# A two-layer diffusion step on one core: parameter loads on ScalarE's queue, the second layer's gate rows through DRAM, and a slack in the order of four kinds of products

## The chip, the cores and the metric

The kernel runs on one core of a Trainium2 chip. The metric is the time of one execution on the device, in microseconds (us). Three runs of the kernel before took 2245.87 us in the median (2241.98 to 2256.99).

## The reference, cut to what matters

Two token sets, 1024 noisy tokens and 256 context tokens, each 1024 wide, go through two layers. Everything is float32.

```
mod   = silu(cond) @ w_ada[layer] + b_ada[layer]       # shift, scale, gate; cond is c or c_ctx
h     = rmsnorm(x, norm_g[layer]) * (1 + scale) + shift
# layer 0: RWKV-7 scan in both directions beside a gated 3-tap convolution
proj  = h @ w_in_e                                     # 1024 x 4352
kk    = k * k_k; kk = kk / max(sqrt(sum_head(kk * kk)), 1e-12)
S     = S * w_t - (S kk_t) (kk_t a_t)^T + v_t k_t^T    # per head 64 x 64, every token, forward and backward
y     = y_f + y_b
y     = (y - mean_head(y)) * rsqrt(var_head(y) + GN_EPS) * lnx_g + lnx_b
bonus = sum_head(r * mean(k_dir) * r_k) * v
x     = x + gate0 * (concat(((y + bonus) * silu(g_a)), conv_branch) @ w_out_e)
# layer 1: grouped-query attention, 16 query heads of 64 on 4 key heads, 512 cached context keys,
# rotary positions, softmax, a SiLU gate on the heads
x     = x + gate1 * ((softmax(q k^T / 8) v * silu(g)) @ w_out_o)
y     = rmsnorm(x, final_g)
```

The gates are vectors of 1024 numbers, one for each token set and layer.

## The kernel before, in words

All values that TensorE multiplies in the large products are split into two float32r parts (`hi`, `lo`), so that each product is three matmuls. The work runs in five stages that overlap at their edges.

1. **Start.** SyncE's queue loads the two conditioning vectors (`crow`), eight tiles of 1 MiB of the first layer's `w_ada` (`wada`, five buffers), four tiles of tokens of 512 KiB (`xt`), and twelve small parameter arrays into the rows of two tiles `prow`, which TensorE turns into columns (`par`). ScalarE forms `cond` from the conditioning vectors; TensorE multiplies it with each `wada` tile as it lands. VectorE turns the sum into the modulation columns (`mod`).
2. **First layer.** The input projection (`mm<-h_hi,whi` and its two companions, weights in pieces of 128 by 128) runs beside the scan. The scan is cut into 20 steps, five for each of four head pairs: four groups of 256 noisy tokens and one for the context. A step is prepared (`prepare`), its triangular systems are built (`interact`), solved on VectorE by 31 pairs of small operations on `acc` and `tmp` (`solve`), put together on TensorE (`merge`) after a trip of the solution through DRAM (`w_d`), and then run through the chain of four blocks (`chain`, tiles `ch`, `py`, `hv`). `close_groups` then normalises y, with the sum over a head as a matmul with the constant `ones2`: once for the mean (operand `y`), once for the squares (operand `sqy`). `norm_k` does the same for the squares of k (operand `sq`), `bonus` for the bonus (operand `kds`).
3. **First output projection** (`Proj` of layer 0, `proj0`): TensorE takes token rows (`omh`) times `w_out_e` (`wts`); VectorE multiplies the result with a gate row (`og<-mm,row`), GpSimd adds x. Behind it comes the turned and modulated h of layer 1 (`all_h1`).
4. **Second layer.** Products with `w_in_o`, then the attention: for each of 24 pairs (two heads, a block of tokens) the scores `qh,kh`, their exponentials on ScalarE (`pe`), the products with the values (`pv<-pe,v_sb`), and the sums of the exponentials (`zs`, on GpSimd and VectorE), which two matmuls add over the partitions (`wk<-zs,twos`).
5. **Second output projection** (`proj1`), the last norm and the stores.

**A gate row** is the gate vector spread over all 128 partitions. `all_rows` makes half of one (512 numbers) at a time, four for a layer: four VectorE operations scale the identity with the gate columns into `dg`, one matmul with the constant `minus` spreads it, and VectorE or ScalarE copies it to `row`.

**What sets the order.** A recording layer (`Loom`) runs all these pieces as generators. Each names what it needs next (`yield "T", operands, rings`), and the loom, with its own costs for the engines, takes the first in a list of precedence (`PRECEDENCE`) that its estimate says could start soon, else the one that could start earliest. What it takes is written into the engines' queues in that order, and the chip runs each queue in order. A need may carry a number, which for an engine other than TensorE is how long another piece may be late to be taken first. The loom works only from the end of the start on; the start is in the order of the program and a priority for the large loads. A `Ring` is a set of buffers that are taken and released; `wk_ps` has two PSUM banks, and one during the attention, since the other goes to the scores. A pool of buffers is opened when the one before is closed: `op0` serves `proj0`, `op1` serves `proj1`.

Names and lines of the kernel before: the loom's `when` is at line 315, the parameter loads at 425 to 446, `norm_k` at 724, `bonus` at 891, `close_groups` at 1253, `all_moved` (the pools) at 1495, `open_proj` at 1602, `all_rows` at 1688. In the profile almost every instruction bears line 145, the loom's own, so they are told apart by the names of their tiles.

Of the kernel before, what the change touches and what calls it, by code (L numbers as in the profile page):

```python
# [17 lines left out]
P = 128  # L18
# [98 lines left out]
class Loom:  # L117
# [199 lines left out]
    def when(self, need):  # L317

        if callable(need):
            return self.clock["T"] if need() else None  # L320
        engines, items, rings, _ = need
        t0 = 0.0
        for x, m in rings.items():
            t = x.ready(m)
            if t is None:
                return None
            t0 = max(t0, t)
        return min(max([t0, self.clock[e]] + [self.free(e, x) for x in items]) for e in engines)

# [38 lines left out]
def hybrid_step(  # L368
# [54 lines left out]
    with tc.tile_pool(name="prm", bufs=2, reuse_waits="tile") as prm:  # L423
        with tc.high_priority():
            crow = prm.tile([16, P], F32, name="crow", bufs=1)
            for i, x in enumerate((c.rearrange("o (n p) -> (o n) p", p=P), c_ctx.rearrange("(n p) -> n p", p=P))):
                dma(out=crow[8 * i:8 * i + 8, :], in_=x)
            pt = py_ps()
            T.transpose(out=pt[:, 0:16], in_=crow, identity=ident[0:16, 0:16])
            V.tensor_copy(par[:, 0:16], pt[:, 0:16])  # L430
        rows["c"], rows["c_ctx"] = 0, 8
        r0 = 0
        t0 = 16
        cur = prm.tile([P, P], F32, tag="prow", name="prow")
        for name, ap, n in specs:
            if r0 + n > P:
                pt = wk_ps()
                T.transpose(out=pt[:, 0:r0], in_=cur[0:r0, :], identity=ident[0:r0, 0:r0])
                V.tensor_copy(par[:, t0:t0 + r0], pt[:, 0:r0])
                t0 += r0  # L440
                r0 = 0
                cur = prm.tile([P, P], F32, tag="prow", name="prow")
            dma(out=cur[r0:r0 + n, :], in_=ap)
            rows[name] = t0 + r0
            r0 += n
        pt = wk_ps()
        T.transpose(out=pt[:, 0:r0], in_=cur[0:r0, :], identity=ident[0:r0, 0:r0])
        V.tensor_copy(par[:, t0:t0 + r0], pt[:, 0:r0])
# [278 lines left out]
    def norm_k(p, b, f, done):  # L727

        t0, n, _ = BLK[b]
        for h in range(0, n, GRP):  # L730
# [3 lines left out]
            S.activation(sq, fh, AF.Square, scale=col("k_k", p))  # L734
            yield "T", sq, wk_ps
            pt = wk_ps.take()
# [158 lines left out]
    def bonus(p, t0, t):  # L895
        yield lambda: passed[f"v{p}"]
        v = st1.tile([P, GRP], F32, tag="vb", name="vb")
        dma(out=v, in_=sp[p][:, 3, t0:t0 + GRP])
        yield "T", t, wk_ps
        pm = wk_ps.take()  # L900
# [352 lines left out]
    def close_groups(x, p, gs):  # L1253
        yield lambda: passed[f"g{p}"]
        sqs, side = [], []
        for t0, y in gs:
# [3 lines left out]
            dma(out=sgt, in_=sg_d[p][:, t0:t0 + GRP])  # L1260
            yield "T", y, iv_ps
            pm = iv_ps.take()
# [6 lines left out]
            S.activation(sq, y, AF.Square)  # L1269
            yield "T", sq, iv_ps  # L1270
            pm = iv_ps.take()
# [201 lines left out]
    k_d = dram.tile([4, NT, C], F32, name="k_d")  # L1473
    v_d = dram.tile([NT, 256], F32, name="v_d")
    m_d = dram.tile([24, P, 32], F32, name="m_d")
    rz_d = dram.tile([24, 2, 512], F32, name="rz_d")
# [22 lines left out]
    def idle(*names):  # L1499
        return not any(R[name].busy for name in names)  # L1500

    def all_moved():
# [26 lines left out]
        close_pool("nx")  # L1529
        yield lambda: len(x1_made) == 2 * N and idle("om", "omh", "og", "xr", "row")  # L1530
        close_pool("op0")
# [70 lines left out]
    def open_proj(name, halves, rows):  # L1602
# [5 lines left out]
        ring(p, "row", [P, 512], rows)  # L1608
        ring(p, "dg", [P, 512], 1)
        if name == "op1":  # L1610
# [28 lines left out]
    def all_wsplit():  # L1639
        for _ in range(len(parts) * KT):  # L1640
# [5 lines left out]
            R["wraw2"].release(raw)  # L1646
            ws[name].append((hi, lo))


    class Proj:  # L1650
# [38 lines left out]
        def all_rows(self):  # L1689
# [3 lines left out]
            for i, h in self.todo:  # L1693
# [3 lines left out]
                seen.append((cd, h))  # L1697
                yield "V", R["dg"], R["row"]
                dg = R["dg"].take()
                row = R["row"].take()  # L1700
                for s in range(4):
                    V.tensor_scalar(out=dg[:, s * P:(s + 1) * P], in0=ident,
                                    scalar1=mods[self.l][:, 16 + h * 4 + s, cd:cd + 1], scalar2=-1.0, op0=ALU.mult, op1=ALU.mult)
                yield "T", dg, wk_ps
                pt = wk_ps.take()
                T.matmul(pt, fixed["minus"], dg, start=True, stop=True)
                R["dg"].release(dg)
                yield from copied(pt, (row, pt))
                wk_ps.release(pt)
                self.rows[cd, h] = row  # L1710
# [694 lines left out]
    def om1_there(i):  # L2405
# [3 lines left out]

    named = dict(chained=all_chained, merged=all_merged, solved=lambda: all_solved(0), solved1=lambda: all_solved(1), finished=all_finished, evac=evacuate,  # L2410
                 loaded=all_loaded, split=all_split, interacted=all_interacted, prepared=all_prepared, x=all_x, h0=lambda: all_h(0), h1=lambda: all_h(1), ada=all_ada,
# [54 lines left out]
```

## Time and profile before

| | |
|---|---|
| median of three runs | 2245.87 us |
| the profiled execution | 2246.71 us |
| its span, first to last instruction | 2245.1 us |
| mean granted TensorE clock | 0.956 of 2.4 GHz |
| TensorE busy | 2044.0 us, 91% |
| VectorE, ScalarE, GpSimd busy | 66%, 47%, 45% |
| moved by DMA | 104 GB/s in the mean |

By the trace, TensorE's first product with a weight of `w_ada` starts at 25 us, the scan runs from 250 to 1167 us, the input projection ends at 1109 us, the first output projection and the products of the second layer fill 1168 to 1523 us, the attention runs to 2126 us, and the last product ends at 2237 us. One reads such a profile by its gaps: 91% busy is a mean over stages, and a gap that one stage has can be filled only by what is ready in that stage. A busy share at a granted clock below 1.00 is also longer than it need be.

### The profile page before, as it was taken

To read this page: it belongs to the slowest core of one execution; us is meant where nothing else is said; L and a number is where in the kernel's file an instruction comes from. 1 tells how busy PE (TensorE), PEld (TensorE's weight loads), DVE (VectorE), ACT (ScalarE), POOL (GpSimd) and SP (SyncE) were. 2 spreads that over 40 slices of the span, in tenths; PEclk is the share of its full clock that TensorE was granted. 3 is DMA by queue.
4 is the path that set the end of the run, shared out by engine and by line. 5 is a ranking of instruction groups with operands and counts; after the bars stand their busy time and mean duration, and the time that the engine had idled before them with its cause. 6 is when DMAs were issued, how large, how long until landed. Compare 5 with 4: busy or idle time off the path is not lost.

```text
span 2245.1 us, 42922 instructions
## 1 busy us (share of the span) xinstructions
PE 2044.0 (91%) x15307; PEld 1406.8 (63%) x15307; DVE 1476.1 (66%) x3483; ACT 1050.0 (47%) x2475; POOL 1013.6 (45%) x1153
## 2 busy tenths in 40 slices
PE   4898889898989999898879999999999999999898
PEld 1486666676666666666657688886544444454487
DVE  3346978858787887878745733555677767775443
ACT  3446647545555456554435632221444444444422
POOL 2434444333344343433224321330587777888622
PEclk8999999899998999999989999999999999999899
DMA  7824434323334343342355633322321211112143
GB/s 290 288 92 137 115 96 125 91 68 107 100 95 108 88 103 93 91 118 54 86 161 183 202 110 90 96 86 89 105 55 45 63 40 36 45 28 75 55 132 107
DMA packets 337817, 232.85 MB, mean 104 GB/s; under 512 B 163890, under 2 KB 289860, under 8 KB 335556
## 3 DMA queue, kind: packets, MB, share of 16 engines
q1 hardware_dynamic: 337604, 230.12, 35.1%
q8 instruction: 120, 1.97, 0.4%
q14 instruction: 93, 0.76, 0.1%
HBM read 166.95 MB, written 57.75 MB: 100 GB/s over the span
## 4 chain that ended last, share of the span: by engine, by line
PE 38%; DVE 10%; DMA 5%; issue 3%; ACT 1%; SPq 1%; POOL 1%; DVEq 0%; POOLq 0%; ACTq 0%
PE mm L145 21%; PE pv L145 8%; PE py L145 5%; PE wk L145 4%; DVE mx L145 3%; DVE rz L145 2%; DVE zs L145 1%; DMA rz<-rz_d 1%; DVE tmp L145 1%; DVE acc L145 1%; SPq L145 1%; DMA rz_d<-rc 1%; PE ch L145 1%; DMA om<-om_d 1%; DVE wts L145 0%
## 5 line engine op out<-in xcount | busy, mean ns | idle before, releaser
L145 POOL TENSOR_TENSOR zs<-zs,pe 128x512 f32<-128x512 f32 x276 | 368.7, 1368 | 43.3 <-ACT pe L145 41.7
L145 PE MATMUL mm<-h_hi,whi 128*128 128x512 f32 (+1 forms) x816 | 336.5, 412 | 4.1 <-ACT whi L145 3.9
L145 PE MATMUL mm<-h_hi,wlo 128*128 128x512 f32 (+1 forms) x816 | 299.1, 366 | 12.6 <-DVE wlo L145 11.7
L145 PE MATMUL mm<-h_lo,whi 128*128 128x512 f32 (+1 forms) x816 | 298.2, 365 | 0.0
L145 POOL TENSOR_TENSOR wlo<-wraw,whi 128x128 fp32r<-128x128 f32 x228 | 110.6, 491 | 242.1 <-ACT whi L145 196.3
L145 PE MATMUL pv<-pe,v_sb 128*64 128x512 f32 (+1 forms) x832 | 203.2, 611 | 0.0
L145 PEld LDWEIGHTS mm<-h_hi,whi 128*128 128x128 f32 x816 | 159.4, 195 | 49.6 <-issue 13.4
L145 PEld LDWEIGHTS mm<-h_hi,wlo 128*128 128x128 f32 x816 | 159.9, 196 | 41.0 <-DVE wlo L145 14.1
L145 DVE TENSOR_TENSOR acc<-acc,tmp 128x60 f32<-128x60 f32 (+23 forms) x620 | 166.9, 271 | 21.0 <-issue 3.1
L145 PEld LDWEIGHTS mm<-h_lo,whi 128*128 128x128 f32 x816 | 160.9, 197 | 14.4
L145 PE MATMUL mm<-wts,omh 128*128 128x512 f32 x624 | 161.0, 409 | 9.1 <-ACT wts L145 5.9
L145 PE MATMUL mm<-wts,h_hi 128*128 128x512 f32 x480 | 151.1, 396 | 0.0
L145 POOL TENSOR_TENSOR hg<-hv,gc 64x128 f32<-64x128 f32 x152 | 65.5, 431 | 188.9 <-DVE hv L145 177.7
L145 DVE TENSOR_REDUCE mx<-py 128x1 f32<-128x512 f32 (+1 forms) x173 | 111.0, 661 | 54.8 <-PE py L145 29.3
L145 PEld LDWEIGHTS mm<-wts,omh 128*128 128x128 f32 x624 | 117.9, 194 | 38.3 <-ACT wts L145 6.8
L145 ACT ACTIVATE whi<-wraw 128x128 fp32r<-128x128 f32 x272 | 80.2, 305 | 81.4 <-PE mm L145 43.7
L145 DVE SCALAR_TENSOR_TENSOR hv<-ch,gc,hg 64x64 f32<-64x64 f32 x288 | 81.3, 282 | 51.6 <-PE ch L145 44.6
L145 ACT ACTIVATE pe<-py 128x512 f32<-128x512 f32 (+1 forms) x139 | 79.4, 586 | 72.6 <-PE mm L145 26.6
L145 POOL TENSOR_TENSOR xr<-xr,og 128x512 f32<-128x512 f32 x40 | 54.6, 1366 | 125.4 <-DVE og L145 91.0
L145 PE MATMUL mm<-h_hi,wts 128*128 128x512 f32 (+1 forms) x384 | 111.1, 364 | 0.0
L145 PEld LDWEIGHTS pv<-pe,v_sb 128*64 128x64 f32 x832 | 51.7, 139 | 93.7 <-issue 81.9
L145 DVE TENSOR_TENSOR tmp<-acc,nra 128x31 f32<-128x31 f32 (+7 forms) x320 | 90.2, 282 | 28.1 <-DMA acc<-eye_d 18.4
(287 smaller groups left out, 5131.2 us busy)
## 6 DMA issues: line engine op xcount, KB each, us to landing
wraw<-in_w_in_e_dram SPq DMA_DIRECT2D x272, 64.0 KB
wada<-in_w_ada_dram SPq DMA_DIRECT2D x16, 1024.0 KB
inp<-rkv_d SPq DMA_DIRECT2D x40, 384.0 KB
om<-om_d SPq DMA_DIRECT2D x52, 256.0 KB
wraw<-in_w_in_o_dram SPq DMA_DIRECT2D x40, 256.0 KB
wada<-in_w_ada_dram SPq DMA_DIRECT2D x16, 512.0 KB
rkv_d<-nb SPq DMA_DIRECT2D x24, 256.0 KB
lor<-lora_d SPq DMA_DIRECT2D x40, 128.0 KB
```

Of the source, the lines that this page charges most:

```text
L145: r = f(*a, **k)
```

## The change

It has three parts.

**Parameter loads.** The twelve loads into `prow` are issued by ScalarE (`nc.scalar.dma_start`) instead of SyncE.

**Gate rows of the second layer.** A new piece, `all_gates`, with its place in the list of precedence behind `rows0`, runs while `op0` is open, once four halves of the first output are stored. It makes each of the four half rows as before (now in `spread`), copies it back into `dg` and stores one partition of it (2 KiB) into a DRAM array `gate_d`. In the second output projection `all_rows` then only loads each half row, broadcast over the partitions. The pool `op0` is held until the four are made, and `op1` has no `dg` any more.

**Slack.** A need of TensorE that carries a number is now taken by the loom as if its operands came that much later. Four needs carry 1.5 (us): the matmuls of `ones2` with `sq`, with `kds` (in `bonus`), with `y` and with `sqy`.

```diff
@@ PRECEDENCE @@
-              ("rows0", 0), ("split0", 0), ("wsplit", 0), ...
+              ("rows0", 0), ("gates", 0), ("split0", 0), ("wsplit", 0), ...
@@ Loom.when @@
-        engines, items, rings, _ = need
+        engines, items, rings, ahead = need
...
-        return min(max([t0, self.clock[e]] + [self.free(e, x) for x in items]) for e in engines)
+        late = ahead if engines == "T" and ahead != 0.6 else 0.0
+        return min(max([t0, self.clock[e]] + [self.free(e, x) + late for x in items]) for e in engines)
@@ parameter loads @@
-            dma(out=cur[r0:r0 + n, :], in_=ap)
+            nc.scalar.dma_start(out=cur[r0:r0 + n, :], in_=ap)
@@ norm_k; bonus; close_groups, twice @@
-            yield "T", sq, wk_ps
+            yield "T", sq, wk_ps, 1.5
-        yield "T", t, wk_ps
+        yield "T", t, wk_ps, 1.5
-            yield "T", y, iv_ps
+            yield "T", y, iv_ps, 1.5
-            yield "T", sq, iv_ps
+            yield "T", sq, iv_ps, 1.5
@@ all_moved @@
-        yield lambda: len(x1_made) == 2 * N and idle("om", "omh", "og", "xr", "row")
+        yield lambda: len(x1_made) == 2 * N and len(gates) == 4 and idle("om", "omh", "og", "xr", "row", "dg")
@@ open_proj @@
-        ring(p, "dg", [P, 512], 1)
+        if name == "op0":
+            ring(p, "dg", [P, 512], 1)
@@ new @@
+    def spread(l, cd, h, row=None):
+        dg = R["dg"].take()
+        for s in range(4):
+            V.tensor_scalar(out=dg[:, s * P:(s + 1) * P], in0=ident,
+                            scalar1=mods[l][:, 16 + h * 4 + s, cd:cd + 1], scalar2=-1.0, op0=ALU.mult, op1=ALU.mult)
+        yield "T", dg, wk_ps
+        pt = wk_ps.take()
+        T.matmul(pt, fixed["minus"], dg, start=True, stop=True)
+        to = dg if row is None else row
+        yield from copied(pt, (to, pt))
+        wk_ps.release(pt)
+        if row is None:
+            dma(out=gate_d[cd:cd + 1, h * 512:(h + 1) * 512], in_=dg[0:1, :])
+        R["dg"].release(dg)
+    def all_gates():
+        yield lambda: len(x1_made) >= 4
+        for cd in range(2):
+            for h in range(2):
+                yield "V", R["dg"]
+                yield from spread(1, cd, h)
+                gates.append((cd, h))
@@ Proj.all_rows @@
-                yield "V", R["dg"], R["row"]
-                dg = R["dg"].take()
... (the lines that are now in spread)
+                if self.l:
+                    yield "D", R["row"]
+                    row = R["row"].take()
+                    dma(out=row, in_=gate_d[cd:cd + 1, h * 512:(h + 1) * 512].broadcast_to([P, 512]))
+                else:
+                    yield "V", R["dg"], R["row"]
+                    row = R["row"].take()
+                    yield from spread(0, cd, h, row)
```

Since the loom orders everything after the start, the slack moves instructions on all engines. Three places are shown.

**The start, SyncE and ScalarE.** Before, the last parameter loads stand in SyncE's queue between the first five and the next three `wada` tiles:

```order
L145 DMA prow<-in_lnx_b_dram 4x128
L145 DMA prow<-in_conv_w_dram 12x128
L145 DMA prow<-in_conv_b_dram 4x128
L145 DMA eye_d<-eye 128x256
L145 DMA wada<-in_w_ada_dram 128x2048 x3
```

Now they stand at the head of ScalarE's queue, ahead of its first squares of the tokens (`xq`) and of `cond`:

```order
L446 DMA prow<-in_lnx_b_dram 4x128
L446 DMA prow<-in_conv_w_dram 12x128
L446 DMA prow<-in_conv_b_dram 4x128
L145 ACT_TABLE_LOAD
L145 ACTIVATE xq,ss<-xt 128x1024
L145 ACT_TABLE_LOAD
L145 ACTIVATE cond<-par 128x8 x2
```

In SyncE's queue the `wada` tiles are now followed by `eye_d` and the next three `wada` alone.

**The end of the input projection, SyncE.** `w_d` and `w` carry the solution of the last scan step through DRAM, `wraw` are the weights of the first output projection. Before:

```order
L145 DMA xr_14120<-in_x_sample_dram 128x512
L145 DMA om_14122<-om_d 128x4x128
L145 DMA wraw_14133<-in_w_out_e_dram 128x512
L145 DMA wraw_14135<-in_w_out_e_dram 128x512
L145 DMA w_d_230<-acc 128x8x32
L145 DMA w_199<-w_d_230 32x8x32 x4
L145 DMA om_d<-y 128x256
```

Now:

```order
L145 DMA w_d_230<-acc 128x8x32
L145 DMA w_199<-w_d_230 32x8x32 x4
L145 DMA vt<-rkv_d_213 128x256
L145 DMA vr<-rkv_d_213 128x256
L145 DMA om_d<-nb_13862 128x512
L145 DMA om_d<-nb_13915 128x256
L145 DMA om_d<-nb_14108 128x512
L145 DMA om_14145<-om_d 128x4x128
```

The last solution now leaves ahead of the last results of the convolution branch (`om_d<-nb`), and the weights come after both.

**The end of the attention, TensorE.** Before, two gate rows and the sums of one pair, between the values of one pair (`pv`) and the next scores (`qh`):

```order
L145 MATMUL pv_23846<-pe_23855,v_sb 64x512
L145 MATMUL wk_23895<-dg_23763,minus 128x512
L145 MATMUL wk_23910<-dg_23902,minus 128x512
L145 MATMUL wk_23921<-zs_23757,twos 64x256
L145 MATMUL wk_23921<-zs_23759,twos 64x256
L145 MATMUL py_23927<-qh_23085,kh_21424 128x512
```

Now:

```order
L145 MATMUL pv_23876<-pe_23882,v_sb 64x512
L145 MATMUL pv_23876<-pe_23885,v_sb 64x512
L145 MATMUL wk_23933<-zs_23794,twos 64x256
L145 MATMUL wk_23933<-zs_23797,twos 64x256
L145 MATMUL py_23938<-qh_23122,kh_21461 128x512
```

The other two rows of `dg` at the end of the attention are gone in the same way, and so are their VectorE operations. The four are now between products of the first output projection, 23 to 32 rows apart in TensorE's order.

## Rows read from the trace of the kernel before

**Rows 1.** The page, busy time, share of the span and instructions of each engine.

```profile
PE 2044.0 (91%) x15307; PEld 1406.8 (63%) x15307; DVE 1476.1 (66%) x3483; ACT 1050.0 (47%) x2475; POOL 1013.6 (45%) x1153
```

**Rows 2.** Busy time by stage; the last three columns: granted clock, DMA share, GB/s.

```profile
105.00:1109.00 1004.00, 909.49 (x9177) 674.86 (x9177) 758.60 (x2183) 549.39 (x1444) 387.16 (x646) 0.95 0.37 99
...
1109.00:1168.00 59.00, 40.23 (x351) 24.72 (x348) 34.63 (x85) 23.65 (x54) 13.94 (x18) 0.83 0.53 159
...
1168.00:1302.00 134.00, 127.95 (x580) 101.69 (x581) 80.18 (x164) 79.73 (x176) 52.28 (x37) 0.99 0.60 187
...
2083.00:2114.00 31.00, 23.65 (x104) 10.80 (x102) 11.95 (x24) 11.74 (x24) 14.32 (x12) 0.78 0.18 53
```

**Rows 3.** Timeline of the start: start, duration, engine, instruction, idle time before and releaser.

```profile
7.58 1.06 ACT L145 ACTIVATE xq<-xt 128x1024 f32<-128x1024 f32 x1 [5.50 <-DMA xt<-in_x_sample_dram]
...
7.95 0.43 SPq L145 DMA_DIRECT2D prow<-in_b_ada_dram  x1
...
10.04 0.32 ACT L145 ACTIVATE cond<-par 128x8 f32<-128x8 f32 x2
...
22.75 0.29 SPq L145 DMA_DIRECT2D prow<-in_conv_b_dram  x1
...
24.14 0.64 PE L145 MATMUL wk<-ident,prow 126*128 126x126 f32 x2 [16.20 <-DMA prow<-in_conv_b_dram]
...
27.04 2.73 SPq L145 DMA_DIRECT2D wada<-in_w_ada_dram  x3
...
38.43 1.93 PE L145 MATMUL wk<-wada,cond 128*32 128x512 f32 x8 [0.63 <-DMA wada<-in_w_ada_dram]
```

**Rows 4.** Busy time by stretch around the pause in the loads of the start.

```profile
14.00:20.00 6.00, 0.00 (x0) 0.00 (x0) 0.00 (x0) 2.21 (x4) 0.00 (x0) 1.00 1.03 424
...
20.00:27.00 7.00, 2.59 (x14) 1.04 (x18) 4.95 (x21) 1.67 (x3) 0.84 (x4) 1.00 0.15 51
```

**Rows 5.** Waits of TensorE, 50 to 1110 us: sum in us, times, longest.

```profile
PE wk L145 <- ACT sq L145: 6.6, 7, 1.9
...
PE iv L145 <- ACT sqy L145: 4.6, 2, 3.7
...
PE iv L145 <- DVE y L145: 2.7, 3, 1.6
```

**Rows 6.** Timeline of SyncE's queue at the end of the scan.

```profile
1115.66 0.38 SPq L145 DMA_DIRECT2D w_d<-acc  x1
...
1121.10 2.50 SPq L145 DMA_DIRECT2D w<-w_d  x4
...
1125.46 0.95 SPq L145 DMA_DIRECT2D wraw<-in_w_out_e_dram  x2
...
1160.34 0.33 SPq L145 DMA_DIRECT2D wraw<-in_w_out_e_dram  x1
```

**Rows 7.** Timeline of TensorE at the end of the attention.

```profile
2081.35 1.94 PE L145 MATMUL pv<-pe,v_sb 128*64 128x512 f32 x8
...
2086.12 1.70 PE L145 MATMUL wk<-dg,minus 128*128 128x512 f32 x2 [2.83 <-DVE dg L145]
...
2088.50 1.97 PE L145 MATMUL wk<-zs,twos 128*64 128x512 f32 x4 [0.69 <-ACT row L145]
...
2102.65 1.13 PE L145 MATMUL wk<-dg,minus 128*128 128x512 f32 x2
...
2106.82 1.93 PE L145 MATMUL wk<-dg,minus 128*128 128x512 f32 x2 [3.05 <-DVE dg L145]
...
2110.58 0.79 PE L145 MATMUL py<-qh,kh 64*128 64x512 f32 x1
...
2125.50 1.13 PE L145 MATMUL wk<-dg,minus 128*128 128x512 f32 x2
```

**Rows 8.** Timeline of VectorE in the first of the two stalls.

```profile
2084.16 1.81 DVE L145 TENSOR_SCALAR dg<-ident,mod 128x128 f32<-128x128 f32 x4
2085.89 0.68 DVE L145 TENSOR_TENSOR zs<-zs,zs 128x512 f32<-128x512 f32 x1
```

More of the change, by code (lines that the diff above doesn't have):

```diff
@@ L53 @@
               ("keyed", 0), ("weighted", 0), ("loaded0", 0.1), ("scored", -0.1), ("done1", 0), ("done2", 0),
[1 row of a table removed]
+              ("rows0", 0), ("gates", 0), ("split0", 0), ("wsplit", 0), ("tables", 1.0), ("rows1", -0.1), ("fill", 0),
               ("projected", 0.5), ("projected1", 1.0))
@@ L1474, in hybrid_step @@
     v_d = dram.tile([NT, 256], F32, name="v_d")
+    gate_d = dram.tile([2, D], F32, name="gate_d")
     m_d = dram.tile([24, P, 32], F32, name="m_d")
@@ L1647, in all_wsplit @@
             ws[name].append((hi, lo))
+    gates = []
+    def spread(l, cd, h, row=None):
[19 more added lines that the diff above has]
+                gates.append((cd, h))
     class Proj:
@@ L1697, in all_rows @@
                 seen.append((cd, h))
-                yield "V", R["dg"], R["row"]
-                dg = R["dg"].take()
[L1700 to L1709, printed above, removed]
+                if self.l:
[6 more added lines that the diff above has]
+                    yield from spread(0, cd, h, row)
                 self.rows[cd, h] = row
@@ L2408, in hybrid_step @@
     proj1 = Proj(1, "last", om1_d, ("o0", "o1"), [(i, (0, 1)) for i in (0, 1, 2, 3, 8, 9, 4, 5, 6, 7)], om1_there, x1_rows, to_y)
-    named = dict(chained=all_chained, merged=all_merged, solved=lambda: all_solved(0), solved1=lambda: all_solved(1), finished=all_finished, evac=evacuate,
+    named = dict(gates=all_gates, chained=all_chained, merged=all_merged, solved=lambda: all_solved(0), solved1=lambda: all_solved(1), finished=all_finished, evac=evacuate,
                  loaded=all_loaded, split=all_split, interacted=all_interacted, prepared=all_prepared, x=all_x, h0=lambda: all_h(0), h1=lambda: all_h(1), ada=all_ada,
```

1 row of the table PRECEDENCE is left out of this document.

## The prediction

> **What bounds the kernel now.** I read the page first, to see which engine is fullest; then the busy time by stage, to see where it is not; then the timelines of the three stages that the change touches. On the page TensorE is busy 91% of the span and no other engine over 66% [rows 1]. So time is to be had only where TensorE stands idle or runs at a lower clock, or where its own work shrinks. By stage [rows 2]: in the first layer (105 to 1109 us) 909 of 1004 us are busy; at its end (1109 to 1168) only 40 of 59, at a mean granted clock of 0.83; in the first output projection and what follows (1168 to 1302) 128 of 134; in a stretch of 31 us at the end of the attention 24, at 0.78. The start is worse: the first 24 us have almost no matmul at all [rows 3].
>
> **Parameter loads.** The reader should see in [rows 3] that TensorE's first real work, the transposes of `prow`, waits 16.20 us for the last of twelve loads of a few KiB. That load was issued at 22.75 and its data was used at 24.14, so it is quick once issued. What is late is the issue: an issue of these takes 0.29 to 0.43 us, yet the twelve take from 7.95 to 22.75, because SyncE's queue has 7 MB of `wada` and `xt` ahead of them, which the DMA moves at 424 GB/s, all it has (share 1.03) [rows 4]. Then the damage is done twice: with the first `wada` tile unused until 25 us, its buffer is free and the sixth tile issued only at 27.04, and DMA falls to 51 GB/s between 20 and 27 us [rows 3, 4]. The eighth tile's products end at 38.43 + 1.93 = 40.36.
>
> On ScalarE's queue the twelve go out from the first microsecond: 12 x 0.29 to 0.43 = 3.5 to 5.2 us, hidden by the 5.50 us for which ScalarE waits for the first tokens [rows 3] (if that cover fails, 1 or 2 us of squares are later, which nothing needs before 40 us). Then `cond`, done at 10.04 + 0.32 = 10.4, is what the products wait for, tiles are used as they land, and the stream does not pause: 8 x 1.05 + 4 x 0.52 = 10.5 MB at 424 GB/s is 24.7 us, from about 2.5 on, so the last tile is there at about 27.5 and used by 29. That is 11 us earlier than 40.36; by the pause alone it would be 7. The bounds are 0 and 11.5. I take **-10**, nearest to the worked-out sum, and carry it to the end, since what follows starts from these columns.
>
> The Trainium skill (DMA: Bandwidth & Descriptors, Issuing engines are not separate DMA queues) speaks against it: all issuers share the same 16 DMA engines, and another issuer saves only the sequencer's time for the issue. By that rule the term is 0. The trace bears it out only in part, since the issue is just what is late here; it is the third rival below.
>
> **The slack of 1.5 us.** It removes nothing; it lets other matmuls pass ahead of these four kinds. TensorE waits for `sq` 6.6 us, for `sqy` 4.6, for `y` 2.7 [rows 5], together 13.9 (that for the bonus is under 1). Where another matmul is ready, that goes; where none is, the loom still issues the product at once. The price is later results: the operand chains (k's norm to the scan, the closing of a step) grow by up to 1.5 us per product, in work that is needed two steps later. And everything after is reordered, which can cost as much as it gives. Bounds: +13.9 to -13.9 with the sign open; clock lost in the stalls (0.95 in the stage [rows 2]) may add some. I take half of the waits, **-7**, as the nearest thing that a row shows.
>
> **The end of the scan.** This is what the reordering does, not what the change says. Before, the last solve is still on VectorE when the input projection ends, and SyncE stands at its store from 1115 on: `w_d` at 1115.66, `w` only at 1121.10, and the third of the sixteen weight tiles of the output projection goes out at 1125.46, the last at 1160.34 [rows 6]. These 14 tiles take 34.9 us, 2.5 each, and their products are what TensorE has in that stage. In the order shown the last solve leaves before the projection ends, so nothing of it stands between the weights: the third tile follows the second by about 2.5 us instead of about 10 (the first two were issued just ahead of 1115.66). That is 7.5 us less if the new place of the solve costs nothing earlier. Bounds: 0 and -18.8, all that TensorE is idle in the stage (59 - 40.2 [rows 2]). I take **-7**.
>
> **Gate rows, made earlier.** Four matmuls at 1.13 us at full clock [rows 7] go into a stretch in which TensorE has 6 of 134 us to spare [rows 2]: **+4.5** on the path. Their VectorE and ScalarE operations are beside a VectorE that is 60% busy; a wait like those of the next paragraph could add up to 3 us each. Stores of 2 KiB and four issues (1.7 us at the dearest issue in [rows 3]) are hidden by SyncE's idle time, and a load of 256 KiB takes well under 1 us at the rate of [rows 4]; without that cover +2.
>
> **Gate rows, no longer made at the end.** In [rows 7] the values of one pair end at 2081.35 + 1.94 = 2083.29 and the next scores start behind the sums, at 2088.50 + 1.97 = 2090.4 (less the overlap of their ends). Between stand 2.83 us waiting for `dg` (VectorE has it behind sums), 1.70 of matmul, 0.69 waiting for the copy (the one bank of `wk_ps`), and the sums, 1.97 at the low clock. Without `dg` the sums still need their last `zs`, which VectorE starts at 2085.89 behind the `dg` of 2084.16 [rows 8]; in the place of that it would end at 2084.16 + 0.68 = 2084.8, and the scores start at 2086.8: 3.6 earlier. At 2102.65 nothing else is between: 2110.58 - 2102.65 less the sums, which take 2110.58 - (2106.82 + 1.93 + 0.78) = 1.05, is 6.9. The fourth matmul gives 1.1. The granted clock is 0.78 in these 31 us, a loss of up to 6.8 us of which I count 2, since by the row of 2110.58 the first score after a stall takes 0.79 [rows 7] and those soon after are quicker again. Together **-13.5**; bounds -8 (the waits and the clock reappear as another wait, only the matmuls and one wait go) and -18.
>
> **Sum.** 2246.7 for the profiled execution (its median sister is 2245.9, 0.8 less, which changes nothing): -10 -7 -7 +4.5 -13.5 = -33, so **2214**.
>
> **The rivals.**
> 1. *The reordering costs what the rest gives in the first layer.* VectorE is busy 759 of the 1004 us [rows 2] and its queue is in order; the new order is as good as another draw. For it: the first chain product stands behind 1146 matmuls instead of 1020 in TensorE's order, 126 more at some 0.11 us each (1004 us for 9177 [rows 2]), 14 us later. Against: the two orders are level again from the ninth step on. Slack +13 instead of -7 and nothing at the end of the scan: -10 +13 +4.5 -13.5, 2241. Chance 0.18.
> 2. *Slack and solve pay in full*, -14 and -15, with the clock: 2199. Chance 0.11.
> 3. *The parameter loads land no earlier*, because the DMA engines serve them behind the megabytes of SyncE: the first term is 0 and the time 2224. For it the share of 1.03 [rows 4], against it the short 1.4 us of the last load. Chance 0.11. This is the skill's rule above.
> 4. *Slower: the scan, not TensorE, sets the length of the first layer.* A step may not run its chain until the step two before it is closed, and closing a group now carries two slacks, 3 us for each of 20 groups. If half of that ends up in the chain, 30 us, and the later first step stays at 14, the time is 2246.7 -10 +44 +4.5 -13.5 = 2272. It decides once closing takes longer than the step in between, some 46 us of the scan's length for each of 20; a slack of 3 is far from it. Chance 0.05.
>
> The forecast itself has 0.55, with 2203 to 2226 as its own range.
>
> **How the numbers follow.** The range goes from 2195 (second rival) to 2240 (most of the first) and leaves out the fourth and the ends. One per cent of the time, about what a measurement of this kernel can tell from no change, is 22 us, so faster means under 2223.4. Faster: nearly all of the forecast (0.50), the second rival, half of the third and a little of the first: 0.68. Within 1%: the rest of these, 0.27. Slower: 0.05.
>
> **What would show it.** Right: `prow` is transposed before 12 us and the eighth `wada` product ends near 29; DMA between 20 and 27 us near 400 GB/s; TensorE's waits for `sq`, `sqy` and `y` sum to less than 7; the third weight tile of the output projection follows the second at once; no gap over 2.5 us between the values and the scores at the end of the attention, and the granted clock there above 0.9. Wrong: parameter loads that land at 20 us, a scan that ends as late as before relative to the start, new waits of TensorE on `ch` or `mm` in the first layer that outweigh those removed, or waits on `dg` between 1168 and 1302.

## The result, and the profile after

The changed kernel takes 2263.31 us (median of nine runs, 2257.4 to 2282.0) against 2243.98 for the kernel before on the same chips: a ratio of **1.0088, interval 1.0062 to 1.0115**, some 20 us slower. 2214 was forecast, with 2240 as the upper end. The profiled execution takes 2260.43 us with a span of 2258.7, so the trace is that of a usual run. Of the runs below, the profiled execution of e15 was a slow one (2503.77 us at a granted clock of 0.731), and neither its time nor its trace is used.

On the page TensorE is as busy as before in share, and every engine has done a few us more [rows 1]:

```profile
PE 2049.0 (91%) x15307; PEld 1411.8 (63%) x15307; DVE 1481.5 (66%) x3494; ACT 1059.7 (47%) x2484; POOL 1019.4 (45%) x1141
```

By stage, busy time of TensorE, weight loads, VectorE, ScalarE and GpSimd, then granted clock, DMA share and GB/s (the first three rows answer to the first three of [rows 2], the last, as long as the last of [rows 2], is the end of the attention):

```profile
105.00:1128.50 1023.50, 904.92 (x9174) 677.38 (x9174) 769.86 (x2207) 561.27 (x1456) 380.16 (x626) 0.94 0.36 95
1128.50:1190.00 61.50, 45.37 (x325) 28.31 (x325) 32.67 (x76) 24.13 (x53) 22.51 (x24) 0.75 0.49 155
1190.00:1325.70 135.70, 128.55 (x580) 100.66 (x579) 82.53 (x178) 80.20 (x178) 56.59 (x39) 1.00 0.56 180
2104.00:2135.00 31.00, 29.91 (x184) 14.62 (x185) 15.34 (x14) 16.88 (x35) 26.63 (x19) 1.00 0.36 107
```

The stretch from 105 us to the end of the input projection is 19.5 us longer with 4.6 us less of TensorE's work in it, though the projection starts 7.2 us earlier. The stall at the end of the attention is gone: 29.9 of 31 us are busy at a granted clock of 1.00, where 23.65 of 31 were at 0.78.

The start (start, duration, engine, instruction, idle time before and releaser; answers to [rows 3]):

```profile
0.80 0.40 ACTq L446 DMA_DIRECT2D prow<-in_b_ada_dram  x1
...
7.67 0.31 ACTq L446 DMA_DIRECT2D prow<-in_conv_b_dram  x1
...
10.68 1.06 ACT L145 ACTIVATE xq<-xt 128x1024 f32<-128x1024 f32 x1 [1.38 <-DMA xt<-in_x_sample_dram]
...
12.93 0.27 PE L145 MATMUL wk<-ident,prow 4*128 4x4 f32 x1 [1.40 <-DMA prow<-in_conv_b_dram]
13.14 0.31 ACT L145 ACTIVATE cond<-par 128x8 f32<-128x8 f32 x2
...
15.50 3.41 SPq L145 DMA_DIRECT2D wada<-in_w_ada_dram  x3
...
33.02 1.06 PE L145 MATMUL wk<-wada,cond 128*32 128x512 f32 x8 [0.97 <-DMA wada<-in_w_ada_dram]
```

The last parameters are used at 12.93 instead of 24.14, the pause in the `wada` stream between 20 and 27 us is gone, and its eighth product ends at 34.1 instead of 40.4. DMA no longer drops there (answers to [rows 4]):

```profile
14.00:20.00 6.00, 4.51 (x24) 0.60 (x16) 1.94 (x7) 2.30 (x4) 0.84 (x4) 1.00 1.01 419
20.00:27.00 7.00, 3.78 (x16) 0.41 (x16) 1.46 (x3) 2.73 (x4) 0.00 (x0) 0.60 1.03 423
```

A shorter pause is new: between 6 and 8 us DMA moves 8 GB/s, where it moved 436 before.

TensorE's waits from 50 to 1130 us (sum in us, times, longest; answers to [rows 5]):

```profile
PE mm L145 <- DVE wlo L145: 24.0, 12, 5.1
...
PE iv L145 <- DVE y L145: 7.8, 7, 2.4
PE iv L145 <- ACT sqy L145: 6.5, 1, 6.5
```

The wait for `sq` has vanished, those for `y` and `sqy` are 14.3 together: the sum is 14.3 against 13.9. TensorE now also waits 24.0 us for the second halves of weights of the input projection (`wlo`). Before, it was less than half of that:

```profile
PE mm L145 <- DVE wlo L145: 11.7, 4, 3.7
```

New waits on `mm` are among the prediction's own signs of being wrong.

### The profile page after: what moved, and what is told of

Same layout as the page of the kernel before. It is cut to its first block, busy times and chain, and to the rows that moved or that the text cites. A ratio compares the mean times of both kernels' runs of the same rounds, so it can differ in the third digit from the quotient of the medians.

```text
span 2258.7 us, 42991 instructions
## 1 busy us (share of the span) xinstructions
PE 2049.0 (91%) x15307; PEld 1411.8 (63%) x15307; DVE 1481.5 (66%) x3494; ACT 1059.7 (47%) x2484; POOL 1019.4 (45%) x1141
## 4 chain that ended last, share of the span: by engine, by line
PE 54%; DVE 20%; DMA 12%; issue 5%; ACT 4%; SPq 3%; POOL 2%; DVEq 0%; POOLq 0%; ACTq 0%
PE mm L145 29%; PE pv L145 7%; PE wk L145 6%; PE py L145 5%; DVE tmp L145 3%; DVE acc L145 3%; PE iv L145 3%; PE ch L145 3%; SPq L145 3%; DVE mx L145 2%; DVE rz L145 2%; DMA rz<-rz_d 1%; DVE hv L145 1%; DMA wada<-in_w_ada_dram 1%; DVE zs L145 1%
## 5 line engine op out<-in xcount | busy, mean ns | idle before, releaser
L145 PE MATMUL mm<-h_hi,whi 128*128 128x512 f32 (+1 forms) x816 | 336.4, 412 | 11.4 <-ACT whi L145 6.3
L145 POOL TENSOR_TENSOR wlo<-wraw,whi 128x128 fp32r<-128x128 f32 x208 | 102.0, 496 | 261.0 <-ACT whi L145 208.8
L145 DVE TENSOR_TENSOR acc<-acc,tmp 128x54 f32<-128x54 f32 (+24 forms) x620 | 170.6, 277 | 17.8 <-issue 1.5
L145 PEld LDWEIGHTS mm<-wts,omh 128*128 128x128 f32 x624 | 119.4, 196 | 43.9 <-ACT wts L145 8.1
```

The source lines that it names most:

```text
L145: r = f(*a, **k)
```

## The experiments

Ratios are to the kernel before on the same chip, with a 95% interval; us are the ratio's distance from 1 times 2247.

| run | what differs from the kernel before | ratio (interval) | us |
|---|---|---|---|
| e1_loads | parameter loads on ScalarE | 0.9958 (0.9937 to 0.9980) | -9 |
| e2_gates | gate rows through DRAM | 0.9980 (0.9957 to 1.0002) | -4.5 |
| e3_slack | slack 1.5 on all four | 1.0158 (1.0117 to 1.0199) | +36 |
| e4_no_slack | loads and gate rows | **0.9939** (0.9909 to 0.9970) | **-14** |
| e5_slack_sq | slack 1.5 on `sq` | 1.0105 (1.0059 to 1.0152) | +24 |
| e6_slack_close | slack 1.5 on `y`, `sqy`, `kds` | 1.0118 (1.0060 to 1.0175) | +27 |
| e7_slack05 | slack 0.5 on all four | 1.0201 (1.0161 to 1.0241) | +45 |
| e8_slack30 | slack 3.0 on all four | 1.0394 (1.0350 to 1.0438) | +89 |
| n1_draw_v | loom's price of VectorE +1 ns | 1.0157 (1.0118 to 1.0197) | +35 |
| n2_draw_s | loom's price of ScalarE -1 ns | 1.0054 (1.0035 to 1.0073) | +12 |
| e9_minus15 | slack -1.5 on all four | 1.0317 (1.0286 to 1.0349) | +71 |
| e10_slack01 | slack 0.1 on all four | 1.0040 (1.0016 to 1.0065) | +9 |
| e11_local15 | slack 1.5 in place, order else as before | 1.0141 (1.0104 to 1.0178) | +32 |
| e12_best | e4 with slack 1.5 in place | 1.0059 (1.0036 to 1.0082) | +13 |
| e13_local30 | slack 3.0 in place | 1.0244 (1.0201 to 1.0287) | +55 |
| e14_local_kds | in place, `kds` alone | 1.0021 (0.9995 to 1.0048) | +5 |
| e15_local_sq | in place, `sq` alone | 1.0087 (1.0058 to 1.0116) | +20 |
| e16_local_close | in place, `y` and `sqy` alone | 1.0038 (1.0014 to 1.0062) | +9 |

### Which part costs

Each part of the change alone, and the change without its slack. Two of the four lines with the number are shown as e4 takes it out; e3 has only the four numbers and the rule in `when`.

```diff
-            yield "T", sq, wk_ps, 1.5
+            yield "T", sq, wk_ps
...
-            yield "T", sq, iv_ps, 1.5
+            yield "T", sq, iv_ps
```

e1_loads. 

> The kernel before with the twelve parameter loads issued by ScalarE and nothing else changed; the order of everything behind the start stays that of before. Theory (the three parts add up; the loads give what the start of the changed kernel gives, its eighth product with a weight of w_ada ending 6.3 us earlier): 6 us faster, 2238. Rival 'the loads land no earlier in effect': no change, 2244. Rival 'the early start is what draws the first layer apart' (it is the loads that cost the 30 us there): 20 us slower, 2264.

e2_gates. 

> The kernel before with the gate rows of the second layer made in the first output projection and loaded from DRAM at the end, loads and slack as before. The order in the first layer is that of before, row for row. Theory: the 10 us that the changed kernel gains behind its 1325 us are these rows, less 4 us for the four matmuls earlier: 6 us faster, 2238 (2234 to 2240). Rival 'the held pool and the earlier matmuls delay the second layer': 5 us slower or more, 2249.

e3_slack. 

> The kernel before with the slack of 1.5 us on all four kinds of products and nothing else; TensorE's order up to the first output projection is then that of the changed kernel, row for row. Theory (the slack alone lengthens the first layer, by later operand chains of the scan): 20 to 30 us slower, about 2269, and the long run of products of the first output projection starts about 30 us later than before. Rival 'slack as predicted': 7 to 14 us faster. Rival 'it costs only together with the earlier start': within 5 us of before.

e4_no_slack. 

> The changed kernel without its slack: the loads on ScalarE and the gate rows through DRAM stay. Theory: 12 to 16 us faster than before, about 2230, so faster than both. Rival 'the parts do not add up': the gain of the loads is lost in the first layer, which waits for something else, and 2238 is left.

e1, e2 and e4 agree with the theory within their intervals, though that of e2 just holds 1, so the gate rows alone are not told from no change. The slack costs a little more than the 20 to 30 us expected. -14 and +36 make +22; the whole change has +20. **The slack is the loss, and without it the change is the fastest version measured, 2231.97 us.**

Where the slack loses is seen when the time is cut where the input projection ends and where the first product of the second layer's weights (`wts,h_hi`) starts. The kernel before:

```profile
62.16:1108.50 1046.34, 947.91 (x9365) 694.25 (x9365) 775.80 (x2214) 570.18 (x1484) 407.45 (x671) 0.95 0.39 107
1108.50:1341.82 233.32, 208.49 (x1156) 161.02 (x1157) 129.29 (x271) 114.61 (x251) 75.16 (x60) 0.95 0.52 163
```

The same two stretches of e3_slack:

```profile
62.45:1135.50 1073.05, 953.48 (x9406) 703.03 (x9406) 788.24 (x2238) 582.56 (x1498) 399.52 (x651) 0.93 0.38 105
1135.50:1369.52 234.02, 210.32 (x1117) 161.82 (x1117) 125.54 (x256) 113.17 (x247) 84.02 (x68) 0.93 0.51 162
```

The stretch with the input projection is 26.7 us longer; TensorE idles 119.6 us in it instead of 98.4 and is 5.6 longer busy, at a lower clock and with 41 more matmuls in it. The next stretch has not changed. So the loss arises in the stretch that the scan fills, and nothing is won at its end. Much of it is there early: the product of `sqy` in the first closing starts at 401.7 us instead of 379.5, and those behind are 12 to 44 us late, without a steady growth.

### Is it the slack, or any new order?

The chain starts at 284 us in e3 instead of 258, since the first two solutions share VectorE: they go to DRAM at 268.4 and 273.5 us instead of 241.8 and 269.6. Theory A makes that the cause, B the chains of operands, C any new draw of the order, D products of the scan that give way to the input projection. Amounts and kinds of slack first:

e5_slack_sq. 

> The kernel before with the slack of 1.5 us on the squares of k (operand sq) alone. In TensorE's order the first chain product again stands behind 1110 matmuls instead of 982, as with all four slacks. In the run with all four, the first two solutions on VectorE ran side by side and went to DRAM at 268.4 and 273.5 us, where before they went at 241.8 and 269.6, and the chain began at 284 instead of 258. Theory A (the slack on sq redraws the order so that the first two solutions share VectorE, the chain starts 25 us late and stays late): 2270 to 2282, nearly all of the 36 us. Theory B (every slack lengthens a chain of operands, the closings of the 20 steps above all, as the slower rival of the prediction had it): under 10 us slower, 2253.

e6_slack_close. 

> The kernel before with the slack of 1.5 us on y, sqy and kds and none on sq. The first chain product stands behind 1000 matmuls, as before (982). Theory A: the chain begins as early as before and the time is within 8 us of before, 2238 to 2254. Theory B (closings): most of the 36 us, 2270 or more. The prediction's own view (waits of TensorE for sqy and y go): up to 7 us faster.

e7_slack05. 

> The kernel before with a slack of 0.5 us on all four. The first chain product stands behind 981 matmuls; the later ones are 170 matmuls later at the third pair. Theory A (what counts is how the new order happens to share VectorE at the start of the scan): within 10 us of before. Theory B (in proportion to the slack): a third of 36, 12 us slower, 2257. Theory C (any change of the order loses, since the one of before is a picked one): 20 us slower or more.

e8_slack30. 

> The kernel before with a slack of 3.0 us on all four. The first chain product stands behind 987 matmuls, the later ones up to 320 matmuls later. Theory A, taken strictly (only the start of the scan counts): within 10 us of before. Theory B (in proportion to the slack): twice 36, 2317. Theory C (any change of the order loses about as much): 2265 to 2285.

A falls: in e6 and e7 the chain starts at 269 us, 15 earlier than in e3 (if 10 later than before), and they lose 27 and 45 us; in e5 it starts later still, at 290, and 24 are lost. B's proportion falls with e7, where a third of the slack costs more than the whole. With 3.0 the loss is larger than any.

Then orders that are new without a meaning, and the slack turned round:

```diff
-COST = {"V": (0.065, 1.04e-3), "S": (0.06, 0.833e-3), "G": (0.15, 2.1e-3)}
+COST = {"V": (0.066, 1.04e-3), "S": (0.06, 0.833e-3), "G": (0.15, 2.1e-3)}
```

n1_draw_v. 

> The kernel before, in which only the loom's own price of a VectorE operation is 0.066 instead of 0.065 us: no slack, no other change, but all orders behind the start come out anew. Theory C (the order of before is a picked one, and any new draw loses 20 to 45 us whatever draws it, the slack of 1.5 us among them): 2265 to 2290. Theory D (the slack itself costs, since it lets products of the input projection pass ahead of the scan, which sets the end): within 10 us of before, 2236 to 2256.

n2_draw_s (0.059 in the place of 0.06). 

> The kernel before, in which only the loom's own price of a ScalarE operation is 0.059 instead of 0.060 us. By its order the last product of the input projection stands at matmul 6069 and the last closing of a step at 6396; before they are at 6189 and 6375. Theory C (any new draw): 2265 to 2290. Theory D (the slack): within 10 us of before.

e9_minus15. 

> The slack of all four kinds turned round to -1.5 us: their products are taken into the order before their operands are there, so that TensorE stands and waits for them. By its order the input projection ends at matmul 6339, behind the last closing of a step (6274). Theory C (any new draw): 2265 to 2290. Theory D (slack starves the scan, so its reverse feeds it): 0 to 15 us faster than before, with waits of TensorE for sq, sqy and y well above the 13.9 us of before. The prediction's view (waits for these operands cost what they last): 10 to 30 us slower through the waits.

e10_slack01. 

> The kernel before with a slack of 0.1 us on all four, an amount that means nothing to TensorE's waits. By its order the first chain product is where it was, the last product of the input projection at matmul 6069 instead of 6189. Theory C (any new draw): 2265 to 2290. Theory D (in the sense and size of the slack): within 10 us of before.

Every new order loses, by 9, 12 and 35 us where nothing but a nanosecond or a tenth of a microsecond asked for it. So a part of C holds, if with a lower bound than expected: only n1 lies in its range, and n2 and e10 are nearer to D's 10 us. Three such draws are few. With -1.5 TensorE's waits for the four operands rise to 24.1 (`sq`), 12.7 (`sqy`), 8.5 (`kds`) and 4.8 (`y`), and 71 us go: the reverse of the slack does not feed the scan, against D's forecast.

### Giving way, with nothing else moved

To part C from D, the order in which the loom of before took its pieces was written down as a string and replayed, with the engines it chose. Only where one of the four kinds would be taken less than the slack behind its operand are the next ready products of the input projection put ahead of it.

```diff
+        for c in TAKEN:
+            i = AL.index(c)
+            if i == dense and passed:
+                passed -= 1
+                continue
+            need = self.live[i][1]
+            if SLACK and not callable(need) and need[0] == "T" and need[3] == 1.5:
+                f = self.live[dense]
+                while f[1] is not None and max(self.free("T", x) for x in need[1]) + SLACK > self.clock["T"]:
...
+                    step(dense)
+                    passed += 1
...
+            step(i)
```

e11_local15. 

> The order of before, written down and replayed, with the slack of 1.5 us applied in place: where one of the four kinds of products would be taken less than 1.5 us behind its operand, the next products of the input projection that are ready are put ahead of it, and everything behind stands as before. TensorE's order differs in 37 places, 868 of 11365 matmuls, and the queues of the other engines and of SyncE do not differ at all. Theory C (the slack as such is harmless or a small gain; the 36 us come from the new draw of all the other queues): between 8 us faster and 3 us slower than before, 2238 to 2249, with TensorE's waits for sq, sqy and y below the 13.9 us of before. Theory D (products of the scan that give way to the input projection delay the scan, wherever they stand): 10 to 36 us slower. The prediction's term: 7 us faster.

e12_best. 

> The same slack in place on the changed kernel without its own slack (loads on ScalarE, gate rows through DRAM, order of before). The version without slack took 0.9939 of before. Theory C: 2224 to 2234, as fast as that version or up to 8 us faster. Theory D: 2242 or more.

e13_local30. 

> As the run with the slack of 1.5 us in place, with 3.0 us: TensorE's order differs in 35 places, 1446 of 11365 matmuls, the other queues in none. When the loom drew the order anew with 3.0 us, the kernel was 87 us slower. Theory C: within 8 us of before. Theory D: 30 us slower or more.

Theory D, clearly. 42 products give way in e11, at 0.8 us each, and the loss grows with the amount: 32 us for 868 displaced matmuls in e11, 55 for 1446 in e13, 0.04 us each in both. The replay with no slack at all was not run, but in e11's trace every engine except TensorE, and SyncE's queue, run through their operations in the order of before. On e4 the same costs 27 us (0.9939 to 1.0059), so the version meant to be best is not. e11's two stretches, cut at the same events:

```profile
62.42:1138.80 1076.38, 953.11 (x9365) 703.65 (x9363) 774.99 (x2214) 570.37 (x1484) 407.22 (x671) 0.94 0.38 104
1138.80:1377.41 238.61, 214.31 (x1157) 164.16 (x1157) 128.43 (x271) 114.49 (x251) 74.84 (x60) 0.91 0.52 160
```

By the counts it is the work of before, and the first stretch takes 30.0 us more, 24.8 of them idle on TensorE; the whole span is 29.7 longer. The product of `sqy` in the first closing is 15 us later than before, that in the twentieth 32 (1193.55 instead of 1161.43), with a nearly steady growth between. How a moved product costs is read on ScalarE, at the first pieces of k's norm. Before (timeline of ScalarE):

```profile
142.35 0.51 ACT L145 ACTIVATE sq<-nb,par 128x256 f32<-128x256 f32 x1 [0.30 <-DVE nb L145]
143.65 0.38 ACT L145 ACTIVATE sq<-wk 128x256 f32<-128x256 f32 x1 [0.79 <-PE wk L145]
...
146.71 0.51 ACT L145 ACTIVATE sq<-nb,par 128x256 f32<-128x256 f32 x1 [1.76 <-DVE nb L145]
148.35 0.39 ACT L145 ACTIVATE sq<-wk 128x256 f32<-128x256 f32 x1 [0.36 <-PE wk L145]
...
151.41 0.51 ACT L145 ACTIVATE sq<-nb,par 128x256 f32<-128x256 f32 x1 [0.24 <-DVE nb L145]
```

And e11_local15:

```profile
143.24 0.51 ACT L266 ACTIVATE sq<-nb,par 128x256 f32<-128x256 f32 x1 [0.63 <-DVE nb L266]
144.53 0.39 ACT L266 ACTIVATE sq<-wk 128x256 f32<-128x256 f32 x1 [0.79 <-PE wk L266]
...
147.59 0.51 ACT L266 ACTIVATE sq<-nb,par 128x256 f32<-128x256 f32 x1 [1.76 <-DVE nb L266]
151.28 0.39 ACT L266 ACTIVATE sq<-wk 128x256 f32<-128x256 f32 x1 [2.39 <-PE wk L266]
...
154.37 0.51 ACT L266 ACTIVATE sq<-nb,par 128x256 f32<-128x256 f32 x1 [1.51 <-DVE nb L266]
```

The squares of a piece (`sq<-nb,par`), TensorE's sum, the root (`sq<-wk`) and VectorE's reciprocal are one loop, since `sq` has a single buffer: the next piece starts when this one is through. The first turn shown, whose product TensorE took at once, takes 4.36 us before and 4.35 in e11; the second 4.70 before and 6.78 in e11, where its root waits 2.39 us for TensorE. What TensorE saves by not waiting, ScalarE and VectorE wait, and the next product of the loop is later by about as much, 2.1 us here. Over 50 to 1150 us the waits behind the moved products read thus, before:

```profile
DVE y L145 <- PE iv L145: 6.8, 8, 1.5
...
DVE sq L145 <- ACT sq L145: 5.7, 5, 2.8
...
ACT sq L145 <- PE wk L145: 2.8, 5, 1.0
```

and in e11_local15:

```profile
DVE y L266 <- PE iv L266: 20.4, 10, 4.5
...
DVE sq L266 <- ACT sq L266: 12.4, 6, 3.9
...
ACT sq L266 <- PE wk L266: 11.1, 11, 2.4
```

These three are 15.3 us before and 43.9 in e11, while TensorE's own waits for `sq`, `sqy`, `y` and `kds` go from 16.6 to 20.2 in the same stretch: the matmuls that pass ahead only put the wait off.

The changed kernel has this mark and another. Its three rows sum to 29.1 us (5.0, 15.9 and 8.2), nearly twice those of before. Its 24.0 us of waits for `wlo` are not of this kind, since e11 has 11.4; n1 and n2, which have no slack, have 22.2 and 22.4 (e10, drawn anew by 0.1 us, has 3.1). So marks of giving way and of a new draw both show in it.

The last three runs ask through what it costs, D1 the chain of the result itself, D2 the in-order queues behind it. All are e11 with the number left on one kind, or on the two of the closing.

e14_local_kds. 

> The slack of 1.5 us in place on the bonus (operand kds) alone: 13 products give way, TensorE's order differs in 14 places, the other queues in none. Nothing needs the bonus before the step is closed. Theory D1 (what costs is the result's own chain: k's norm to the scan, the closing of a step): 0 to 2 us slower. Theory D2 (what costs is that VectorE and ScalarE stand at the operation that reads the late product, with all that is queued behind it, whatever the result is for): in proportion to the 42 products and 30 us of the run with all four, 9 us slower, 2257.

e15_local_sq. 

> The slack of 1.5 us in place on the squares of k (operand sq) alone: 15 products give way, TensorE's order differs in 14 places, the other queues in none. Theory D1: half of the 30 us or more, 15 to 20 us slower, since k's norm feeds the scan. Theory D2: 11 us slower, 2259.

e16_local_close. 

> The slack of 1.5 us in place on y and sqy: 19 products give way, TensorE's order differs in 18 places, the other queues in none. Theory D1: 10 to 15 us slower, the rest of the 30. Theory D2: 14 us slower, 2262. The prediction's view: up to 4 us faster, half of TensorE's 7.3 us of waits for these two.

15 products of `sq` cost 20 us, 1.3 each; 19 of `y` and `sqy` 9, 0.45 each; 13 of `kds` 5, 0.36 each, with an interval that holds both zero and D2's 9. The sum is 33 (before rounding), against 32 with all, though 47 products give way in the three and 42 in e11. That `sq` costs most is D1, whose 15 to 20 it meets while D2's 11 lies below its interval (13 to 26 us), and the loop above is how. For `y` and `sqy` the interval (3 to 14) holds most of D1's range and D2's value; whether the in-order queues take a share of their own is left open by `kds`.

## Why the prediction was wrong

1. **The slack is the step that failed.** The prediction put it at -7, half of TensorE's 13.9 us of waits [rows 5], because "where another matmul is ready, that goes", and because the later results are needed only "two steps later". It measures +32 in place (23 to 40) and +36 as written (26 to 45). The waits did not go: they are 14.3 in the changed kernel. Nor was the delay free: a product of k's norm has its next consumer in line at once, in a loop over one buffer, and in the turn shown the root waits 2.0 us longer and the turn takes 2.1 longer.
2. **The new order costs as well.** The three orders drawn anew for no reason lose 9 to 35 us, so that of before is a good one among its neighbours. The prediction called the new order "as good as another draw" and gave that 13 us in its first rival; another draw is worse than the one that is there. How the 36 us of the slack as written divide between giving way and the new draw stays open: in place the order is not new, but every new order also moves these products, and the changed kernel bears the marks of both.
3. **The end of the scan**, -7 in the prediction, gave nothing. The third weight tile was to follow the second at once. After, SyncE's queue reads:

```profile
1135.68 0.43 SPq L145 DMA_DIRECT2D wraw<-in_w_out_e_dram  x1
1141.79 0.34 SPq L145 DMA_DIRECT2D wraw<-in_w_out_e_dram  x1
...
1181.01 0.33 SPq L145 DMA_DIRECT2D wraw<-in_w_out_e_dram  x1
```

   The second to the third takes 6.1 us, but the third to the last 39.2 instead of 34.9 [rows 6]; the stretch up to the second layer takes 234.0 us in e3 against 233.3. The solution was out of the way, but the queue waited 13.2 us for the last `nb`, until 1131.31, and its stores now stand ahead of the weights. So the first weight tile goes out at 1134.27, 5.8 us behind the end of the input projection, as before (1114.43, 5.9 behind it). From there on the waits for the splits of the weights (`wts`) are 13.0 us, against 15.0 in the 53 us from 1112 on before; new are 5.4 us at the stores of the scan's states (`s_out`), and 5.6 instead of 2.9 for the splits of token rows (`omh`).
4. **Parameter loads**: the mechanism is right. The input projection starts at 56.6 us in e1 and 55.0 after, against 62.2, so 5.6 to 7.2 earlier and less than the -10 forecast; the time of e1, -9 (-14 to -4), does not exclude -10. The stream did not pause between 20 and 27 us, but its eighth product ended at 34.1 and not at 29: the new pause between 6 and 8 us is in it, and SyncE issued its fifth tile at 11.62 instead of 7.58. The sum counted 24.7 us of stream at the full rate from 2.5 us on and had no such pause. The rival that the loads land no earlier falls: they went through a queue of their own and were used 11 us earlier, while DMA stayed at 419 to 423 GB/s. The last one took longer, though, 5.3 us from issue to use instead of 1.4. The rule of the Trainium skill (DMA: Bandwidth & Descriptors, Issuing engines are not separate DMA queues), that all issuers run on the same 16 DMA engines and another one saves only the time of the issue, agrees with the trace on the bandwidth, which the second issuer did not raise (424 before); the issue is what counted here.
5. **Gate rows earlier**, +4.5: the stretch from the end of the input projection to the second layer is 240.0 us in e2 and 237.1 in e4 against 233.3, so +4 to +7. Over the six traces with the order of before in that stretch and the four with the rows it is 234.5 and 238.1 in the mean, +3.7. Waits on `dg` there, which the prediction had among its signs against it, sum to 4.8 us after (at most 1.6) and to 3.2 before.
6. **Gate rows at the end**, -13.5: from the second layer to the end of the span it is 903.3 us before, 890.2 in e2, 887.0 in e4 and 892.4 after, so 11 to 16 less. One trace of before is not much to go by, since this stretch varies by 10 us between kernels that keep their gate rows: it is 896.8 to 906.3 in fifteen traces of such kernels, 901.3 in the mean, against 887.0 to 892.4 in the four with rows from DRAM, 889.7 in the mean. That is 11.6 less. TensorE at the end of the attention, after (answers to [rows 7]):

```profile
2105.03 1.94 PE L145 MATMUL pv<-pe,v_sb 128*64 128x512 f32 x8
2108.06 2.11 PE L145 MATMUL wk<-zs,twos 128*64 128x512 f32 x4 [1.09 <-DVE zs L145]
2110.10 0.49 PE L145 MATMUL py<-qh,kh 64*128 64x512 f32 x1
```

   From the end of the values at 2106.97 to the scores it is 3.1 us instead of 7.1, and the first score takes 0.49 instead of 0.79. This step was about right in its size, though no run has it without step 5; the two together are e2's -4.5, whose interval (-14 to +0.4) holds their -9.
7. **Of the rivals**, the slower one (2272, chance 0.05) had the sign and half of the mechanism: the scan sets the length of the first layer. It looked at the closings, which in place are the smaller part (9 us against 20 for `sq`), and held a slack of 3 to be far from the point at which the scan decides. 1.5 in place already costs 32. The first rival (2241, chance 0.18) had the order cost 13; the redraws bear that out in kind.

Steps 4 to 6 sum to -19 in the prediction and measure -14 in e4. The rest, -14 forecast for the slack and the end of the scan and +36 measured, is nine tenths of the miss.

## What to carry to other kernels

The end of a wait of the busiest engine is no saving by itself: look for who reads the result and what stands behind the reader before letting other work pass ahead. In this kernel the product in a loop over a single buffer is better taken when its operand is there, even though the fullest engine stands still for it at times; taken 1.5 us ahead of its operand, with a new order, it cost more still (e9). And where an order comes out of a planner that was tuned, test a planner's rule against redraws that mean nothing, and in place with every other queue fixed; only the second tells the rule's own cost.

## What the runs showed of the hardware

With two engines issuing at the start, neither issued steadily: in the trace of the changed kernel SyncE's third issue came at 4.89 us instead of 1.68, and ScalarE's ninth parameter load at 6.69, 2.6 us behind the end of its eighth. Before, SyncE issued nine transfers between 0.80 and 4.95 without a gap above 0.1 us. The trace puts SyncE's waits down to parameter loads of ScalarE that were still on their way (3.2 us for `norm_g`, 1.7 for `mu_shift`), and in e1, e4 and e12, the other kernels with these loads on ScalarE, it shows the same two waits (2.9 to 3.2 and 1.4 to 1.7 us). No run tests why an issue of one engine should wait for a load of the other.
